# Depthwise convolutions, key norm and decay series: operands taken from and kept in PSUM

## The chip, the cores and the metric

One core of a Trainium2 chip runs the whole program in one launch. The metric is the device time of one execution in microseconds. The engines are named as in the profile: PE (matmul; PEld its weight load), DVE (VectorE), ACT (ScalarE), POOL (GpSimd), SP (its DMA queue). SBUF is the on-chip memory that all engines use; PSUM is the small one that PE writes its products to, in 8 banks of 512 fp32 columns. POOL has no PSUM operand in this kernel; DVE and ACT have.

## What is computed

A two-layer encoder on 256 tokens of width 1024. Each layer has a mixer of three parallel branches (dense attention A, neighbourhood attention B, gated DeltaNet C) and a top-2 mixture of 32 experts. The change lies in branch C's convolution and decay, and in branch A's key norm:

```python
p = h @ w_in
(aq, ak, av, bq, bk, bv, cq, ck, cv, cz, cbf, cbb, caf, cab, gate) = _split_cols(p, IN_SPLITS)
...
k = _axial_rope(_rms(k, k_g), tables)
...
qkv = jax.nn.silu(_short_conv(jnp.concatenate([q, k, v], axis=-1), conv_w))
...
g = -jnp.exp(A_log[d].astype(F32)) * jax.nn.softplus(aa.astype(F32) + dt_bias[d].astype(F32))
```

`_short_conv` is a centred convolution of 5 taps along the tokens, channel by channel. `g` is the log decay of the chunked delta rule, of 16 values per token partition.

## The kernel before

A layer runs as a mixer stage and an expert stage. The mixer's input projection takes `w_in` in column blocks in the order of `ORDER` (L50): first a block of gates (`ga0`), then branch C's queries and keys (`cqk`), its gate and decay inputs (`cz`), its values (`cv`), branch A's keys and values (`akv`), its queries (`aq`), and so on. Each block comes in four units of 256 rows. A unit is loaded by SP, its rounded half `uh_...` is made by ACT and the remainder `ul_...` by DVE or POOL (`split`, L185; `POOL`, L42, lists the units whose remainder POOL makes), and PE takes three products of them (`mm3`, L188). Four buffers of each kind go round.

PE's order is pinned as the program is recorded: `projections` (L1040) yields after every few products, and `pump` (L328) lets side lines put their matmuls between them. `delta_line` (L607), `key_line` (L581) and `query_line` (L593) are such lines. The order on DVE, ACT and POOL is a scheduler's, and each of them works its own queue strictly in order.

The steps that the prediction follows:

- `conv` (L536): ACT copies a PSUM bank of products into SBUF (`ring0` or `ring1`, both in the place H), DVE applies 5 taps to each of two channel groups (`ts`, then four `stt`), ACT takes a tanh into the ring, DVE forms `cs`. It runs three times, for `cqk` twice and for `cv`.
- `norm_rope` (L554): ACT copies the products to a ring, squares them, DVE reduces, POOL raises to the power -1/2 (`rsqrt`, L228), DVE scales, POOL multiplies by the sines, DVE by the cosines and adds. For the keys (`which` = 1) it runs for two token tiles. The second tile uses `ring0` and `ring1`, as the third convolution uses `ring0`.
- The decay series (L630 to L646): some 25 DVE instructions of 16 columns in the tile `gap`, which end in `g`. POOL then multiplies `g` with triangles three times (L656), PE forms `eb` and `db` from them (L662, L685), and then transposes the keys (`kTA`, L590).
- The query's norm (L596) follows the last `aq` product; PE transposes its result as `qTA` (L602).

PSUM banks come from three pools (`BANKS`, L155): `acc` with 3, `one` with 1, `s` with 4.

Of the kernel before, what the change touches and what calls it, by code (L numbers as in the profile page):

```python
# [15 lines left out]
OP = mybir.AluOpType  # L16
# [5 lines left out]
S = 256  # L22
# [91 lines left out]
def kernel(ctx: ExitStack, tc: tile.TileContext, a: dict, out: bass.AP):  # L114
# [45 lines left out]
    def tt(eng, o, x, y, op):  # L160
        return eng.tensor_tensor(out=o, in0=x, in1=y, op=op).ins  # L161
# [145 lines left out]
    def mixer(l, fetch, norm):  # L307
# [74 lines left out]
        def of(n, *shape):  # L382

            names = "abcd"[:len(shape)]
            w = where[n][:, :int(np.prod(shape))]
            if len(shape) == 1:
                return w
            return w.rearrange(f"p ({' '.join(names)}) -> p {' '.join(names)}", **dict(zip(names, shape)))
# [146 lines left out]

        def conv(i, b):  # L536

            bv = of(f"ring{i % 2}", 2, S)
            with tc.high_priority(offset=PRI):
                A.copy(bv.rearrange("p m s -> p (m s)"), b)  # L540
            y = of(f"cy{i % 2}", 2, S)
            for m in range(2):
                ch = 2 * i + m
                ts(V, y[:, m], bv[:, m], cw[:, ch, 2:3], OP.mult)
                for j in (0, 1, 3, 4):
                    s = j - 2
                    t0, t1 = max(0, -s), S - max(0, s)
                    stt(y[:, m, t0:t1], bv[:, m, t0 + s:t1 + s], cw[:, ch, j:j + 1], y[:, m, t0:t1],
                        OP.mult, OP.add)
            A.activation(bv, y, AF.Tanh)  # L550
            stt(cs[i], bv, 1.0, y, OP.add, OP.mult)


        def norm_rope(b, t, n, which, dst, name):  # L554

            turn = 2 * (t + which) % 4
            x, y = of(f"ring{turn}", 512), of(f"ring{turn + 1}", 512)
            A.copy(x[:, :n * 64], b)
            xv = x8(x[:, :n * 64])
            sq = y  # L560
            A.activation(sq[:, :n * 64], x[:, :n * 64], AF.Square)
            rs = of(f"rs{t}", 8)
            V.tensor_reduce(out=rs[:, :n], in_=x8(sq[:, :n * 64]), axis=AX.X, op=OP.add)
            rsqrt(rs[:, :n], rs[:, :n], 1.0 / 64.0, 1e-6, n)
            tt(V, xv, xv, rs[:, :n, None].to_broadcast([128, n, 64]), OP.mult)
            yv = x8(y[:, :n * 64])
            s5 = gc_[:, which, 1, t].rearrange("p (a b e) -> p a b e", a=2, b=2)
            for b_ in range(2):
                o = y[:, :n * 64].rearrange("p (h a b e) -> p h a b e", a=2, b=2, e=16)[:, :, :, b_]
                i0 = x[:, :n * 64].rearrange("p (h a b e) -> p h a b e", a=2, b=2, e=16)[:, :, :, 1 - b_]  # L570
                i1 = s5[:, None, :, b_].to_broadcast([128, n, 2, 16])
                tt(G, o, i0, i1, OP.mult)
            tt(V, xv, xv, gc_[:, which, 0, t:t + 1].to_broadcast([128, n, 64]), OP.mult)
            tt(V, dst, xv, yv, OP.add)
# [32 lines left out]
        def delta_line(vbank, zb):  # L607
# [19 lines left out]

                return ap8.rearrange("p (d h) -> p d h", d=2)[:, :, None, :].to_broadcast([128, 2, 2, 4])

            xx, ax, ee, rr, ss, pp, acc, g = (sc[:, i] for i in range(8))  # L630
            tt(V, xx.rearrange("p (d t h) -> p d t h", d=2, t=2), ba[:, 1], dh(al[:, 1]), OP.add)
            stt(ax, xx, -1.0, xx, OP.mult, OP.max)
            A.activation(ee, ax, AF.Exp, scale=-1.0)
            ts(V, rr, ee, 2.0, OP.add)
            V.reciprocal(rr, rr)
            tt(V, ss, ee, rr, OP.mult)
            tt(V, pp, ss, ss, OP.mult)
            ts(V, acc, pp, 1.0 / 19.0, OP.mult)
            for k in range(17, 1, -2):
                stt(acc, acc, 1.0 / k, pp, OP.add, OP.mult)  # L640
# [399 lines left out]
        def projections():  # L1040
            for i, n in enumerate(ORDER):
                if n == XFREE:
                    free("X")
                if n == RSPAWN:
                    spawn("router", router_line(), RLAG)
                if n == "cqk":
                    bs = [bank("acc", f"cqk{l}{i}") for i in range(2)]
                    for u in range(4):
                        uh, ul = take()
                        for k in range(2):  # L1050
                            chan(bs, uh, ul, u, k, 0, 4)
                            yield
                    conv(0, bs[0])
                    conv(1, bs[1])
                elif n == "cz":
                    zb = [bank("acc", f"cz{l}{t}") for t in range(2)]
                    for u in range(4):
                        uh, ul = take()
                        for k in range(2):
                            for t in range(2):  # L1060
                                mm3(zb[t][:, :272], act(2 * u + k, t), (uh[:, k], ul[:, k]),
                                    u == 0 and k == 0, u == 3 and k == 1)
                            yield
                elif n == "cv":
                    vbank = bank("acc", f"cv{l}")
                    for u in range(4):
                        uh, ul = take()
                        for k in range(2):
                            chan([vbank], uh, ul, u, k, 0, 2)
                            yield  # L1070
                    spawn("delta", delta_line(vbank, zb))
                elif n == "akv":
                    spawn("key", key_line((yield from token_major(n, 256))))
                elif n == "aq":
                    spawn("query", query_line((yield from token_major(n, 512))))
                elif n == "bqk":
                    bs = [bank("acc", f"bqk{l}{i}") for i in range(2)]
                    for u in range(4):
                        uh, ul = take()
                        for k in range(2):  # L1080
                            chan(bs, uh, ul, u, k, 0, 4)
                            yield
                    for i in range(2):
                        A.copy(bqk[:, i].rearrange("p m s -> p (m s)"), bs[i])
                elif n == "bv":
                    bs = yield from token_major(n, 256)
                    for t in range(2):
                        A.copy(vB[:, t], bs[t])
                    done.add("b")
                else:  # L1090
                    bs = yield from (token_major(n, 512) if i else tile_by_tile(n))
                    if i == 0:
                        small_inputs()
                    key = n[1], int(n[2])
                    if key not in gth:
                        pair = gc if n[1] == "c" else st((128, 2, 2, 512), "gb", f"gb{l}")
                        gth[n[1], 0], gth[n[1], 1] = pair[:, 0], pair[:, 1]
                    for t in range(2):
                        A.activation(gth[key][:, t], bs[t], AF.Tanh, scale=0.5)
# [531 lines left out]
```

## Time and profile before

| what | value |
|---|---|
| median of 3 runs | 1470.63 us (1470.15 to 1471.12) |
| the profiled execution, its own time | 1470.02 us |
| its span, first to last instruction | 1468.4 us |
| PE busy | 1341.5 us, 91% of the span |
| DVE, ACT, POOL busy | 632.3, 403.8, 266.2 us |
| mean granted clock of PE | 0.972 |
| HBM read | 476.40 MB |

The 1.6 us between the time and the span lie before the first and behind the last instruction. Times in the views count from the start of the span. A timeline row gives start, duration, engine, line, operation, output, inputs and shape; in brackets stands how long the engine was idle before and what ended that. `placeA`, `placeB`, ... are 2048-column places in SBUF that hold several named tiles; which one is meant follows from the line. The first mixer fills about 0 to 283 us, the second about 740 to 1010 us.

### The profile page before, as it was taken

Reading aid. Unit: us, or ns where it says so; the run is one execution under the profiler, and the core shown is the slowest. Engines: PE = TensorE matmul, PEld = TensorE weight load, DVE = VectorE, ACT = ScalarE, POOL = GpSimd, SP = SyncE. Lnnn points to the kernel's source line nnn. Section 1 sums busy time; section 2 is a strip of 40 time slices with the busy share of each in tenths; the row PEclk is TensorE's granted clock in tenths of the full one; section 3 lists DMA queues with packets and bytes.
Section 4 is the critical chain, followed back from the end, with each engine's and each line's share of the span. In section 5 each row is a group of like instructions: output and inputs, shape, how many; then the busy total and the mean of one; then the engine's idle time right before and its main releaser. Section 6 shows DMA issues by size and latency. Waiting matters only on the chain. (4 is left out here: it accounts for less than half of the span.)

```text
span 1468.4 us, 23692 instructions
## 1 busy us (share of the span) xinstructions
PE 1341.5 (91%) x9708; PEld 893.4 (61%) x9708; DVE 632.3 (43%) x1214; ACT 403.8 (28%) x769; POOL 266.2 (18%) x327
## 2 busy tenths in 40 slices
PE   6889999799998999999678799997999899999986
PEld 5768777555554555555367677774555556555542
DVE  6887667622221222222169875775222212222213
ACT  3445543211111111211134455332211111111111
POOL 4485304300000000000036743033000000000000
PEclk9999999899999999999979899999999999999999
DMA  7535779699999999999655457796999999999995
GB/s 232 168 123 148 226 244 344 233 405 419 419 419 417 419 419 419 419 419 420 266 163 156 138 141 255 242 355 239 407 418 419 418 418 419 420 419 419 419 419 212
DMA packets 114533, 479.89 MB, mean 327 GB/s; under 512 B 25168, under 2 KB 38000, under 8 KB 65520
## 3 DMA queue, kind: packets, MB, share of 16 engines
q1 hardware_dynamic: 112464, 471.85, 82.7%
q0 software_dynamic: 1376, 5.24, 1.0%
q8 instruction: 81, 1.33, 0.4%
q10 hardware_dynamic: 576, 1.18, 0.2%
q14 instruction: 36, 0.29, 0.1%
HBM read 476.40 MB, written 1.84 MB: 326 GB/s over the span
## 5 line engine op out<-in xcount | busy, mean ns | idle before, releaser
L176 PE MATMUL h<-w,h 128*64 128x256 f32 x2016 | 232.7, 387 | 21.7 <-PEq L1382 9.5
L176 PEld LDWEIGHTS h<-w,h 128*64 128x64 f32 x2016 | 144.0, 139 | 100.3 <-issue 16.6
L170 DVE SCALAR_TENSOR_TENSOR hid<-hid,h 128x256 f32<-128x256 f32 x64 | 27.0, 421 | 401.3 <-ACT hid L1473 401.3
L170 DVE SCALAR_TENSOR_TENSOR op<-mo,rt,op 64x512 fp32r<-64x512 f32 x128 | 95.9, 749 | 223.0 <-ACT op L1500 222.0
L1500 ACT ACTIVATE op<-mo,rt 64x512 fp32r<-64x512 f32 x128 | 87.4, 683 | 314.5 <-PE mo L176 275.1
L176 PE MATMUL mo<-w,hidT 128*64 128x512 f32 x720 | 164.3, 595 | 3.5 <-DMA w<-in_w_dram 2.2
L161 POOL TENSOR_TENSOR W<-P,rt 128x128 f32<-128x128 f32 x64 | 24.2, 399 | 785.2 <-PE PT L182 710.3
L1473 ACT ACTIVATE hid<-h 128x256 f32<-128x256 f32 x64 | 24.6, 385 | 402.3 <-PE h L176 402.3
L176 PEld LDWEIGHTS mo<-w,hidT 128*64 128x64 f32 x720 | 50.7, 137 | 89.1 <-issue 77.3
L176 PE MATMUL h<-w,xg 128*64 128x256 f32 x864 | 96.9, 380 | 2.3 <-ACT h L1448 2.3
L176 PE MATMUL h<-wl,h 128*64 128x256 f32 x768 | 86.3, 381 | 2.1 <-ACT h L1448 1.4
L176 PEld LDWEIGHTS h<-w,xg 128*64 128x64 f32 x864 | 61.0, 137 | 33.6 <-ACT h L1448 3.4
L176 PE MATMUL mo<-wl,hidT 128*64 128x512 f32 x304 | 69.8, 597 | 2.5 <-DMA wl<-in_w_dram 2.5
L176 PEld LDWEIGHTS h<-wl,h 128*64 128x64 f32 x768 | 53.9, 137 | 29.9 <-ACT h L1448 2.1
L176 PE MATMUL my<-op,PT 128*128 128x512 f32 x256 | 69.7, 412 | 2.1 <-ACT op L1500 1.4
L176 PE MATMUL xg<-P,hh 128*128 128x256 f32 x256 | 56.4, 303 | 5.8 <-DVE P L161 5.8
L176 PEld LDWEIGHTS my<-op,PT 128*128 128x128 f32 x256 | 45.5, 188 | 25.4 <-issue 11.5
L176 PEld LDWEIGHTS xg<-P,hh 128*128 128x128 f32 x256 | 40.8, 196 | 29.6 <-issue 29.5
L176 PE MATMUL xg<-P,hl 128*128 128x256 f32 x256 | 52.7, 288 | 0.0
L176 PE MATMUL h<-wl,xg 128*64 128x256 f32 x416 | 47.7, 382 | 3.2 <-DMA wl<-in_w_dram 1.6
L176 PEld LDWEIGHTS mo<-wl,hidT 128*64 128x64 f32 x304 | 20.6, 137 | 37.3 <-issue 29.8
L176 PE MATMUL wo<-uh_wo,ym 128*128 128x512 f32 x128 | 41.4, 395 | 0.0
(436 smaller groups left out, 2463.9 us busy)
## 6 DMA issues: line engine op xcount, KB each, us to landing
w<-in_w_dram SPq DMA_DIRECT2D x268, 1024.0 KB, 19.9
wl<-in_w_dram SPq DMA_DIRECT2D x112, 1024.0 KB, 19.9
w_gb<-in_w_in_dram SPq DMA_DIRECT2D x16, 512.0 KB, 3.7
w_gc<-in_w_in_dram SPq DMA_DIRECT2D x16, 512.0 KB, 4.5
w_wo<-in_w_out_dram SPq DMA_DIRECT2D x16, 512.0 KB, 4.8
w_ga<-in_w_in_dram SPq DMA_DIRECT2D x14, 512.0 KB, 4.7
w_cqk<-in_w_in_dram SPq DMA_DIRECT2D x8, 512.0 KB, 3.7
w_aq<-in_w_in_dram SPq DMA_DIRECT2D x8, 512.0 KB, 4.5
```

Source lines behind the costliest of these rows:

```text
L161: return eng.tensor_tensor(out=o, in0=x, in1=y, op=op).ins
L170: return V.scalar_tensor_tensor(out=o, in0=x, scalar=s, in1=y, op0=op0, op1=op1)
L176: ins = T.matmul(o, l, r, start=start, stop=stop, skip_group_check=True).ins
L1473: A.activation(u, b[:, :256], AF.Tanh, scale=0.5)
L1500: A.activation(hi, src, AF.Copy, scale=w)
```

## The change

The three convolutions read their products where PE left them and write their tanh back there; the copy into the ring is gone. The key norm squares and scales straight from PSUM and writes the scaled key to the ring; the query norm stays as it was. The decay series keeps its reciprocal, one of two copies of its quotient and its running sum in a PSUM bank `sb`, and forms the square from one factor in PSUM and one in SBUF, which is one instruction more. The banks of `cqk` and `cv` come from the pool `s` in place of `acc`.

```diff
         def conv(i, b):
 
-            bv = of(f"ring{i % 2}", 2, S)
-            with tc.high_priority(offset=PRI):
-                A.copy(bv.rearrange("p m s -> p (m s)"), b)
+            bv = b.rearrange("p (m s) -> p m s", m=2)
             y = of(f"cy{i % 2}", 2, S)
...
             turn = 2 * (t + which) % 4
             x, y = of(f"ring{turn}", 512), of(f"ring{turn + 1}", 512)
-            A.copy(x[:, :n * 64], b)
             xv = x8(x[:, :n * 64])
+            raw = x8(b) if which else xv
+            if not which:
+                A.copy(x[:, :n * 64], b)
             sq = y
-            A.activation(sq[:, :n * 64], x[:, :n * 64], AF.Square)
+            A.activation(sq[:, :n * 64], b if which else x[:, :n * 64], AF.Square)
             rs = of(f"rs{t}", 8)
             V.tensor_reduce(out=rs[:, :n], in_=x8(sq[:, :n * 64]), axis=AX.X, op=OP.add)
             rsqrt(rs[:, :n], rs[:, :n], 1.0 / 64.0, 1e-6, n)
-            tt(V, xv, xv, rs[:, :n, None].to_broadcast([128, n, 64]), OP.mult)
+            tt(V, xv, raw, rs[:, :n, None].to_broadcast([128, n, 64]), OP.mult)
...
-            xx, ax, ee, rr, ss, pp, acc, g = (sc[:, i] for i in range(8))
+            xx, ax, ee, ss, pp, g = (sc[:, i] for i in range(6))
+
+            sb = bank("s", f"sb{l}")
+            rr, sq_, acc = (sb[:, 16 * i:16 * i + 16] for i in range(3))
             tt(V, xx.rearrange("p (d t h) -> p d t h", d=2, t=2), ba[:, 1], dh(al[:, 1]), OP.add)
             stt(ax, xx, -1.0, xx, OP.mult, OP.max)
             A.activation(ee, ax, AF.Exp, scale=-1.0)
             ts(V, rr, ee, 2.0, OP.add)
             V.reciprocal(rr, rr)
+            tt(V, sq_, ee, rr, OP.mult)
             tt(V, ss, ee, rr, OP.mult)
-            tt(V, pp, ss, ss, OP.mult)
+            tt(V, pp, sq_, ss, OP.mult)
             ts(V, acc, pp, 1.0 / 19.0, OP.mult)
...
-                    bs = [bank("acc", f"cqk{l}{i}") for i in range(2)]
+                    bs = [bank("s", f"cqk{l}{i}") for i in range(2)]
...
-                    vbank = bank("acc", f"cv{l}")
+                    vbank = bank("s", f"cv{l}")
```

PE's order is the same before and after. On the other three the scheduler places things anew. First DVE, in the middle of the series, in the kernel before (`gap` is the series, `placeA` the third convolution's sum, `placeH` the ring, `placeS` small tiles with the taps, `ul_aq` a remainder of a query unit):

```order
L161 TENSOR_TENSOR gap_83<-gap_83 128x16
L165 TENSOR_SCALAR placeA_99<-placeH_105,placeS_108 128x256
L161 TENSOR_TENSOR gap_83<-gap_83 128x16
L165 TENSOR_SCALAR placeA_99<-placeH_105,placeS_108 128x256
L165 TENSOR_SCALAR gap_83<-gap_83 128x16
L170 SCALAR_TENSOR_TENSOR placeA_99<-placeH_105,placeS_108,placeA_99 128x254
L170 SCALAR_TENSOR_TENSOR gap_83<-gap_83 128x16
L170 SCALAR_TENSOR_TENSOR placeA_99<-placeH_105,placeS_108,placeA_99 128x254
L186 TENSOR_TENSOR ul_aq_657<-w_aq_571,uh_aq_656 128x1024
```

The first query remainder stands behind the quotient, the square and one step of the series, and each instruction around it has both tensors in SBUF. The same stretch with the change:

```order
L165 TENSOR_SCALAR placeA_99<-cv_495,placeS_108 128x256
L170 SCALAR_TENSOR_TENSOR placeC_100<-cqk_276,placeB_98 128x512
L186 TENSOR_TENSOR ul_akv_638<-w_akv_550,uh_akv_637 128x512
L170 SCALAR_TENSOR_TENSOR placeG_106<-placeG_106,cz_421 128x256
L170 SCALAR_TENSOR_TENSOR placeG_106<-placeG_106,cz_422 128x256
L186 TENSOR_TENSOR ul_aq_656<-w_aq_569,uh_aq_655 128x1024
L167 TENSOR_SCALAR placeS_108<-placeS_108 128x16
L165 TENSOR_SCALAR sb_588<-gap_83 128x16
L170 SCALAR_TENSOR_TENSOR placeA_99<-cv_495,placeS_108,placeA_99 128x254
L638 RECIPROCAL sb_588<-sb_588 128x16
```

The remainder now stands ahead of the whole series, and the third convolution's first tap ahead of it, on the bank `cv` that PE must have finished. Second POOL, from the last query remainder to the end of the keys, in the kernel before (L232 is the power, `placeH` the ring, `placeG` and `placeC` the triangles):

```order
L186 TENSOR_TENSOR ul_aq_737<-w_aq_672,uh_aq_736 128x1024
L232 TENSOR_TENSOR placeS_108<-placeS_108,mhalf 128x2
L161 TENSOR_TENSOR placeH_105<-placeH_105,placeA_99 128x4x16 x2
L161 TENSOR_TENSOR placeG_106<-gap_83,placeK_109 128x512 x2
L161 TENSOR_TENSOR placeC_100<-gap_83,placeK_109 128x512
L232 TENSOR_TENSOR placeS_108<-placeS_108,mhalf 128x2
```

and with the change:

```order
L186 TENSOR_TENSOR ul_aq_734<-w_aq_671,uh_aq_733 128x1024
L232 TENSOR_TENSOR placeS_108<-placeS_108,mhalf 128x2
L161 TENSOR_TENSOR placeH_105<-placeH_105,placeA_99 128x4x16 x2
L161 TENSOR_TENSOR placeG_106<-gap_83,placeK_109 128x512
L232 TENSOR_TENSOR placeS_108<-placeS_108,mhalf 128x2
L161 TENSOR_TENSOR placeG_106<-gap_83,placeK_109 128x512
L161 TENSOR_TENSOR placeC_100<-gap_83,placeK_109 128x512
L161 TENSOR_TENSOR placeH_105<-placeH_105,placeA_99 128x4x16 x2
```

The second key tile's power has moved ahead of the second and third triangle. Its sine products stay behind all three.

## Rows read from the trace of the kernel before

**Rows 1.** Windows: stretch, length, PE, PEld, DVE, ACT, POOL busy, clock, DMA share, GB/s
```profile
40.00:80.00 40.00, 35.16 (x215) 30.08 (x213) 36.95 (x76) 18.16 (x33) 23.61 (x16) 0.96 0.53 158
80.00:120.00 40.00, 32.87 (x214) 29.10 (x214) 33.35 (x69) 17.72 (x29) 27.66 (x21) 0.87 0.43 129
120.00:160.00 40.00, 39.23 (x228) 30.55 (x226) 28.15 (x49) 24.43 (x52) 24.06 (x48) 1.00 0.64 180
...
280.00:300.00 20.00, 18.51 (x143) 13.04 (x143) 3.96 (x10) 2.25 (x6) 1.10 (x3) 0.88 0.53 184
...
500.00:600.00 100.00, 98.52 (x722) 58.00 (x720) 24.89 (x48) 18.57 (x39) 2.27 (x6) 1.00 1.01 419
```

**Rows 2.** Waits of PE, 0 to 270 us: in total, times, longest
```profile
PE qTA L182 <- DVE placeE L161: 4.9, 2, 3.5
PE aq L176 <- DVE ul_aq L186: 3.2, 1, 3.2
PE kTA L182 <- ACT gap L668: 2.3, 1, 2.3
```

**Rows 3.** Timeline of PE, three places in layer 1, then two in layer 2
```profile
53.45 0.28 PE L176 MATMUL akv<-uh_akv,placeT 128*128 128x256 f32 x1
...
82.19 0.66 PE L182 MATMUL kTA<-cst,placeG 128*128 128x128 f32 x4 [2.34 <-ACT gap L668]
...
109.01 0.90 PE L182 MATMUL qTA<-cst,placeE 128*128 128x128 f32 x3 [3.53 <-DVE placeE L161]
...
811.93 0.66 PE L182 MATMUL kTA<-cst,placeG 128*128 128x128 f32 x4 [1.73 <-ACT gap L668]
...
838.69 0.90 PE L182 MATMUL qTA<-cst,placeE 128*128 128x128 f32 x3 [3.38 <-DVE placeE L161]
```

**Rows 4.** Timeline of DVE, 60 to 86 us
```profile
60.74 2.35 DVE L170 SCALAR_TENSOR_TENSOR gap<-gap 128x16 f32<-128x16 f32 x1
...
63.41 1.21 DVE L186 TENSOR_TENSOR ul_aq<-w_aq,uh_aq 128x1024 fp32r<-128x1024 f32 x1
...
72.32 0.17 DVE L165 TENSOR_SCALAR gap<-gap 128x16 f32<-128x16 f32 x1
...
74.75 1.01 DVE L165 TENSOR_SCALAR gap<-gap,placeK 128x16 f32<-128x16 f32 x1
...
85.08 0.68 DVE L161 TENSOR_TENSOR placeB<-placeB,placeK 128x512 f32<-128x512 f32 x1
```

**Rows 5.** Timeline of POOL, 60 to 76 us
```profile
60.38 2.69 POOL L186 TENSOR_TENSOR ul_aq<-w_aq,uh_aq 128x1024 fp32r<-128x1024 f32 x1 [1.28 <-ACT uh_aq L186]
...
71.34 0.73 POOL L232 TENSOR_TENSOR placeS<-placeS,mhalf 128x2 f32<-128x2 f32 x1 [3.52 <-DVE gap L170]
72.55 1.13 POOL L161 TENSOR_TENSOR placeH<-placeH,placeA 128x64 f32<-128x64 f32 x2 [0.47 <-DVE gap L165]
73.64 2.09 POOL L161 TENSOR_TENSOR placeG<-gap,placeK 128x512 f32<-128x512 f32 x2
```

**Rows 6.** Timeline of ACT: the second key tile's copy in and copy out
```profile
73.53 0.27 ACT L558 COPY placeH<-akv 128x128 f32<-128x128 f32 x1 [0.74 <-DVE placeC L170]
...
81.72 0.30 ACT L585 COPY placeG<-placeG 128x128 f32<-128x128 f32 x1 [2.50 <-DVE placeG L161]
```

**Rows 7.** Timelines of DVE and POOL at 116.7 us: one operand in PSUM beside POOL
```profile
116.68 0.28 DVE L161 TENSOR_TENSOR placeC<-placeF,gr 128x128 f32<-128x128 f32 x1
...
116.71 1.29 POOL L161 TENSOR_TENSOR placeA<-placeC,placeK 128x512 f32<-128x512 f32 x1 [5.38 <-DVE placeC L161]
```

**Rows 8.** Groups of DVE by form, whole span: count, busy us, mean ns, idle before
```profile
L170 DVE SCALAR_TENSOR_TENSOR gap<-gap 128x16 f32<-128x16 f32 x22 | 12.4, 565 | 0.1
...
L170 DVE SCALAR_TENSOR_TENSOR placeA<-placeH,placeS,placeA 128x254 f32<-128x254 f32 x16 | 7.6, 476 | 0.0
...
L170 DVE SCALAR_TENSOR_TENSOR placeH<-s_b,placeE 128x256 f32<-128x256 f32 x16 | 6.0, 415 | 0.1
...
L170 DVE SCALAR_TENSOR_TENSOR lg<-lg,stats,bwr 128x32 f32<-128x32 f32 x4 | 1.0, 254 | 0.0
```

## The prediction, made blind

> **What bounds the kernel now.** I read the windows first. In the expert stage the DMA share is 1.01 at 419 GB/s, so that stage is bound by loading its weights. In the mixer the share is about half, and PE works 39 of 40 us from 120 us on, but only 35 and 33 of 40 between 40 and 120 us, with DVE busy for 37 and 33 [rows 1]. So the mixer has slack on PE in one stretch, and DVE is full there. Between the stages, at 280 to 300 us, the DMA share is 0.53: the prefetched experts are waiting and nothing is queued for memory. Whatever the mixer saves therefore starts the expert stream earlier, and its fixed length ends earlier by as much.
>
> The waits say what PE stands for in that stretch: the query transpose 4.9 us, the first query product 3.2, the key transpose 2.3, nearly all of it on DVE [rows 2]. The PE timeline then shows which of them count. From the key transpose of layer 1 to that of layer 2 it is 729.74 us, and from query transpose to query transpose 729.68, though the waits ahead of them differ [rows 3]. So the arrival of keys and queries sets the time, not the waits before: a wait at the first query product that goes away only moves PE sooner to the key transpose.
>
> Last, DVE and POOL side by side. A series step of 16 columns takes 2.35 us at 60.74, and POOL's remainder runs from 60.38 to 63.07: DVE ends as POOL does [rows 4, 5]. A step without such company takes 0.17 [rows 4], yet 22 steps average 0.565 [rows 8]. DVE instructions with two tensors in SBUF wait out POOL's. Those with one tensor in PSUM do not: at 116.68 one takes 0.28 while a POOL product starts at 116.71 and lasts 1.29 [rows 7].
>
> **The change, part by part.** *Removed:* five ACT copies per layer (three convolution banks, two key tiles). ACT is busy 18 of 40 us [rows 1]; by itself that is worth nothing, since ACT's casts there wait for PE, DVE or a transfer. What counts is that the second key tile no longer needs the ring: its copy at 73.53 waited for the third convolution's last DVE instruction [rows 6]. *Banks:* `eb` and the three `db` now take over the four banks of `cqk`, `cv` and `sb`. They need `g`, which DVE makes after the last read of each of these banks, so no wait is added: nothing. *The extra product* of the series: 0.17 us on DVE, counted below.
>
> *Step one, the time of `g`.* The first tap of the third convolution waits for PE to end `cv`, now 53.45, where the first key product starts [rows 3]; with POOL unhindered a little earlier, so I take 53.0. Behind it stand a 512-column step (0.68), two gate steps and the tap (0.42 each, the 256-column PSUM row), half a remainder (0.6) and the first query remainder (1.21): 3.8, so 56.8 [rows 4, 8]. From there to `g` the new DVE order has 19 instructions of 16 columns or fewer at 0.17 = 3.2, nine convolution steps at 0.42 = 3.8, one of 512 columns 0.68, four key steps of 128 columns at 0.42 or less = 1.7, and four remainders at 1.21 = 4.8. That is 14.2, and `g` is ready at 71.0, against 72.3 [rows 4]. The four remainders are the part that can still wait for POOL, and each needs PE to have freed its buffer. First gain: 1.3, if PE is not late for `eb`, and without its wait at the first query product it is not.
>
> *Step two, from `g` to the key transpose.* Now it is 9.9 us (72.3 to 82.19), because the second key tile starts at 73.53 and one half of the decay is held up for 1.01 [rows 3, 4, 6]. With the change the chain is POOL's: three triangles at 1.05 = 3.1, the power 0.73 between them, two sine products 1.13 [rows 5], then two DVE steps (0.6), the copy out (0.30) and six hand-overs at 0.2, about the 0.17 between that copy's end and the transpose [rows 3, 6]: 7.1. The key transpose comes at 78.1 instead of 82.19. Gain so far: 4.1.
>
> *Step three, from there to the query transpose.* Before, DVE starts the masks of branch C 2.9 us behind the key transpose (85.08), as the decay factors and one remainder stand ahead [rows 3, 4]. With the change these are placed before the last key step, and the masks can start when ACT has the exponentials, about 0.6 behind the transpose (an exponential of 512 columns, put at DVE's 0.68 for that width, starts with the hand-over to PE): 2.3 sooner. I take 2.2, since the query's squares on ACT may then come last. All that follows to the query transpose (109.01) is the same DVE and POOL queue, moved as a whole. PE, only 4.1 earlier, still waits there, for 4.9 − 2.2 = 2.7. Gain per layer: 6.3.
>
> The rest of the mixer is PE work that follows the query transpose at the same distance, and the solve on POOL that starts from it moves along. The clock is 0.96 and 0.87 in the two windows [rows 1], low after the idle stretches; one shorter stretch may give back a microsecond, one longer (PE waiting for `g`) take it: nothing. The second layer repeats the first [rows 3]. Two layers: 12.6, and 1470.02 − 12.6 = 1457.4 for the profiled execution. The median of the runs is 0.6 above that execution, so I forecast 1458.
>
> [...] The nearest PSUM row, 256 columns, takes 415 ns, and the SBUF row of 254 columns 476 [rows 8]: PSUM is no dearer there. [...]
>
> **The rivals.**
> *Small PSUM steps are dear.* No row shows a 16-column step in PSUM. The nearest, 32 columns read and written in PSUM, takes 0.254 [rows 8] against 0.17. If all 30 PSUM instructions between 53 us and `g` cost 0.08 more, `g` is 2.4 later: gain 3.9 per layer, 1462. For it: the row is the only one of that size. Against: the larger ones are not dearer.
> *Slower.* If a dependent step through PSUM costs about as much as a row of 512 columns, 0.68 [rows 4], the 17 chained steps of the series are 0.5 dearer each, 8.7 in all. The key transpose is then 4.6 later than now, step three gives 2.2 back, and two layers lose 5: 1475. It decides from 0.37 more per step on (6.3 / 17). Nothing in the trace is that dear, and the steps alternate with convolution steps that hide part of it.
> *PSUM operands take turns with POOL all the same.* Then `g` stays at 72.3 and only the ring's release counts: 2.8 + 2.2 per layer, 1460. Rows 7 speak against it.
> *Nothing arrives.* If the expert stream were waiting for memory already in the mixer, or a later wait took the gain back, it is 1470. Against: the DMA share of 0.53 before the stream, and a PE that is full from 120 us on [rows 1].
> *More.* If DVE's backlog goes altogether, all three waits vanish, 10.4 per layer [rows 2]: 1449.
>
> **How the numbers follow.** Forecast with the rival at 1460, 1453 to 1461: 0.58. Small steps dear, 1461 to 1466: 0.18. More, 1444 to 1452: 0.11. Nothing: 0.07. Slower: 0.06. Runs of this kernel differ by 0.07%, and a measurement can tell about 0.2%, 2.9 us, from no change. Faster: 0.58 + 0.18 + 0.11 = 0.87; same 0.07; slower 0.06. The range 1449 to 1465 leaves out no change, slower, and the outer ends of the two neighbours of the forecast.
>
> **What would show it.** Right: series steps and convolution steps at 0.2 and 0.45 with no 2 us outliers; no wait at the first query product; the key transpose near 78 and the query transpose near 102.7, still waiting; the same distances in layer 2. Step one is wrong if `g` is not near 71, two if it takes other than 7 us to the key transpose, three if DVE's masks do not follow within 1 us. The whole is wrong if the series' PSUM steps exceed 0.5, or if the expert stage grows by what the mixer loses.

## The result and the profile after

The changed kernel takes 1455.13 us (median of 4 runs, 1453.57 to 1456.89) against 1470.63: a ratio of 0.9892, 95% interval 0.9878 to 0.9905, so 15.5 us less. The profiled execution took 1453.57 us with a span of 1451.9. The forecast was 1458 and its range held the time.

The windows of [rows 1], in the kernel after:

```profile
40.00:80.00 40.00, 37.02 (x227) 32.28 (x226) 36.25 (x94) 20.04 (x37) 22.44 (x20) 0.91 0.63 194
80.00:120.00 40.00, 36.28 (x257) 32.73 (x256) 32.60 (x62) 18.41 (x34) 24.33 (x17) 0.91 0.39 117
...
280.00:300.00 20.00, 18.52 (x150) 11.01 (x151) 4.69 (x10) 3.50 (x8) 0.00 (x0) 1.00 0.93 335
```

PE works 37.0 and 36.3 of 40 us, where it worked 35.2 and 32.9. DVE is hardly less busy: it does more in the same time. From 280 us on the expert stream already runs (DMA share 0.93, before 0.53).

PE's timeline, places that answer to [rows 3], then the first of its waits up to 270 us behind the loads at the program's start, to be read with [rows 2]:

```profile
52.26 0.28 PE L176 MATMUL akv<-uh_akv,placeT 128*128 128x256 f32 x1
...
70.71 2.74 PE L176 MATMUL eb<-gap,placeK 128*128 128x8 f32 x12 [2.98 <-DVE gap L165]
73.29 3.63 PE L176 MATMUL db<-placeG,placeK 128*128 128x512 f32 x4
...
77.61 0.60 PE L182 MATMUL kTA<-cst,placeG 128*128 128x128 f32 x4
...
101.52 0.90 PE L182 MATMUL qTA<-cst,placeE 128*128 128x128 f32 x3 [3.53 <-DVE placeE L161]
...
822.46 0.55 PE L182 MATMUL qTA<-cst,placeE 128*128 128x128 f32 x3 [2.54 <-DVE placeE L161]
```

```profile
PE qTA L182 <- DVE placeE L161: 3.5, 1, 3.5
...
PE eb L176 <- DVE gap L165: 3.0, 1, 3.0
```

The query transpose comes 7.49 us sooner in layer 1 (109.01 to 101.52), and 16.23 in layer 2 (838.69 to 822.46). That is nearly the whole gain: the span is 16.5 shorter. Some 0.5 us of it is an earlier start of this execution (PE's first products begin at 10.02 instead of 10.56) and not the change. The waits at the first query product and at the key transpose are gone; one at `eb` is new.

DVE's timeline after, for [rows 4]:

```profile
51.79 1.17 DVE L165 TENSOR_SCALAR gap<-gap 128x16 f32<-128x16 f32 x1
...
62.10 0.17 DVE L170 SCALAR_TENSOR_TENSOR sb<-sb,gap 128x16 f32<-128x16 f32 x1
62.22 1.05 DVE L167 TENSOR_SCALAR placeS<-placeS 128x2 f32<-128x2 f32 x1
...
69.08 1.22 DVE L186 TENSOR_TENSOR ul_ga<-w_ga,uh_ga 128x1024 fp32r<-128x1024 f32 x1
...
70.49 0.16 DVE L165 TENSOR_SCALAR gap<-gap 128x16 f32<-128x16 f32 x1
...
77.58 0.69 DVE L161 TENSOR_TENSOR placeB<-placeB,placeK 128x512 f32<-128x512 f32 x1 [1.45 <-ACT placeB L690]
```

`g` is at 70.49 (72.32 before), the first mask (a triangle multiplied into branch C's decay factors) at 77.58 (85.08). From `g` to the mask it is 7.09 us instead of 12.76. Three remainders of the gate units, the last of them the row at 69.08, now stand ahead of `g`; before, all three stood between `g` and the masks (75.68, 79.36 and 81.60, 1.2 us each). ACT shows the other half. First two rows of the kernel before, then four of after:

```profile
77.97 0.30 ACT L585 COPY placeG<-placeG 128x128 f32<-128x128 f32 x1 [2.89 <-DVE placeG L161]
...
81.92 0.22 ACT L668 ACTIVATE gap<-eb 128x64 f32<-128x64 f32 x1
```

```profile
69.11 0.30 ACT L585 COPY placeG<-placeG 128x128 f32<-128x128 f32 x1 [0.88 <-DVE placeG L161]
73.48 0.22 ACT L672 ACTIVATE gap<-eb 128x64 f32<-128x64 f32 x1 [4.08 <-PE eb L176]
...
76.17 0.30 ACT L585 COPY placeG<-placeG 128x128 f32<-128x128 f32 x1 [0.19 <-DVE placeG L161]
76.95 0.60 ACT L690 ACTIVATE placeB<-db 128x512 f32<-128x512 f32 x1 [0.49 <-PE db L176]
```

Before, ACT copied both key tiles out (77.97, and 81.72 of [rows 6]) ahead of the exponential of `eb`, which PE had ready at 77.2 and which ran at 81.92; ahead of each of these copies ACT stood for DVE (2.89 and 2.50 us). After, the first key tile is done ahead of `g`, the exponential follows `eb` at once, and the second tile comes behind it.

Where DVE found the room stands in its groups by form, 36 to 83 us, of before and then of after:

```profile
L170 DVE SCALAR_TENSOR_TENSOR gap<-gap 128x16 f32<-128x16 f32 x11 | 6.2, 561 | 0.0
L170 DVE SCALAR_TENSOR_TENSOR placeB<-placeH,placeS,placeB 128x255 f32<-128x255 f32 x4 | 4.0, 991 | 0.0
L170 DVE SCALAR_TENSOR_TENSOR placeB<-placeH,placeS,placeB 128x254 f32<-128x254 f32 x4 | 3.9, 995 | 0.0
```

```profile
L170 DVE SCALAR_TENSOR_TENSOR placeB<-cqk,placeS,placeB 128x254 f32<-128x254 f32 x4 | 1.9, 474 | 0.0
L170 DVE SCALAR_TENSOR_TENSOR placeB<-cqk,placeS,placeB 128x255 f32<-128x255 f32 x4 | 1.9, 473 | 0.0
...
L170 DVE SCALAR_TENSOR_TENSOR sb<-sb,gap 128x16 f32<-128x16 f32 x10 | 1.7, 171 | 0.0
```

The second convolution loses 4.1 us (7.9 to 3.8), the series 4.5. Both were waits for POOL (experiments 1, 2 and 8), and POOL waited as well. Its remainders of the `cv` units in the kernel before, and the first of the same three after:

```profile
44.95 7.13 POOL L186 TENSOR_TENSOR ul_cv<-w_cv,uh_cv 128x512 fp32r<-128x512 f32 x3 [9.64 <-ACT uh_cv L186]
```

```profile
44.41 1.29 POOL L186 TENSOR_TENSOR ul_cv<-w_cv,uh_cv 128x512 fp32r<-128x512 f32 x1 [9.45 <-ACT uh_cv L186]
```

### The profile page after: what moved, and what is told of

Its sections match the earlier page's. It is cut to its first block, busy times and chain, and to the rows that moved or that the text cites. A ratio compares the mean times of both kernels' runs of the same rounds, so it can differ in the third digit from the quotient of the medians.

```text
span 1451.9 us, 23681 instructions
## 1 busy us (share of the span) xinstructions
PE 1337.3 (92%) x9708; PEld 893.7 (62%) x9708; DVE 618.6 (43%) x1216; ACT 400.5 (28%) x759; POOL 254.7 (18%) x327
```

## The experiments

**Theory:** the operands in PSUM free DVE of POOL; with that room, work that stood behind `g` moves ahead of it. **Rivals:** the ring's release of the second key tile alone; the order on ACT; a wait that only moves to the next instruction. PE's first products begin at 10.0 to 11.2 us in these profiles, so a few tenths between two of them are the start. From the masks to the query transpose of layer 1 it was 23.8 to 24.0 us in the runs of experiments 1 to 10, but for 23.1 in the first and 23.4 in the fifth; so the masks tell when the queries come.

**1. The convolutions alone** (`conv_only`): the kernel before, with the convolutions' part of the diff.

```diff
-            bv = of(f"ring{i % 2}", 2, S)
-            with tc.high_priority(offset=PRI):
-                A.copy(bv.rearrange("p m s -> p (m s)"), b)
+            bv = b.rearrange("p (m s) -> p m s", m=2)
...
-                    bs = [bank("acc", f"cqk{l}{i}") for i in range(2)]
+                    bs = [bank("s", f"cqk{l}{i}") for i in range(2)]
```

> Only the three convolutions read PSUM; series and key norm as before. Theory (port): DVE steps with two operands in SBUF wait out POOL's, one operand in PSUM avoids it. Then the convolution steps all take 0.47 us, the ring is free early, but the series keeps one or two steps of some 2 us beside POOL's query remainders; g comes 2 us later than with the whole change and the key and query transposes too: 1459 us. Rival (only the ring's release counts, the places of operands do not): 1455, as the whole change. Rival (the series carries the gain): 1468.

Measured 1456.67 us, 0.9904 [0.9888, 0.9919]. DVE's timeline:

```profile
58.79 1.48 DVE L161 TENSOR_TENSOR gap<-gap 128x16 f32<-128x16 f32 x1
...
61.72 2.37 DVE L161 TENSOR_TENSOR gap<-gap 128x16 f32<-128x16 f32 x1
...
72.09 0.16 DVE L165 TENSOR_SCALAR gap<-gap 128x16 f32<-128x16 f32 x1
...
73.97 2.06 DVE L186 TENSOR_TENSOR ul_ga<-w_ga,uh_ga 128x1024 fp32r<-128x1024 f32 x1
...
79.31 0.69 DVE L161 TENSOR_TENSOR placeB<-placeB,placeK 128x512 f32<-128x512 f32 x1
```

The convolutions bring 14 of the 15.5 us, although the series still waits (1.48, 2.37) and `g` is only 0.2 sooner than before, which is the start (10.36 against 10.56). One gate remainder is left behind `g` instead of three, and the mask comes 7.2 us behind it. The time lies between the theory's 1459 and the 1455 of the first rival and does not choose between them; experiments 5 and 6 do. The edit also takes the copies away: DVE's idle time ahead of the first tap falls from 1.5 us (behind ACT's copy) to 0.9 (behind PE), so that the first copy is worth some 0.6 us and not the 4.1 above.

**2. The series alone** (`series_only`): the kernel before with the bank `sb` and the steps in it.

```diff
-            xx, ax, ee, rr, ss, pp, acc, g = (sc[:, i] for i in range(8))
+            xx, ax, ee, ss, pp, g = (sc[:, i] for i in range(6))
+
+            sb = bank("s", f"sb{l}")
+            rr, sq_, acc = (sb[:, 16 * i:16 * i + 16] for i in range(3))
...
+            tt(V, sq_, ee, rr, OP.mult)
             tt(V, ss, ee, rr, OP.mult)
-            tt(V, pp, ss, ss, OP.mult)
+            tt(V, pp, sq_, ss, OP.mult)
```

> Only the decay series keeps operands in PSUM; convolutions and key norm go through the ring as before. Theory (port): the series' steps take 0.17 us, but the convolution steps that stand between them meet POOL's remainders instead and take 2 us; the ring is not released; 1468 us, g within 1 us of its time before. Rival (the series' stalls are the cause): g 4 us earlier, 1462.

Measured 1469.48, 0.9995 [0.9986, 1.0003]: nothing. Every step in the bank takes 0.17 (the reciprocal 0.27), but `g` is at 73.99, 1.7 later than before and not within 1 as expected. The waits went to the taps beside it (at 60.26 one of 2.57 us with two tensors in SBUF, at 64.95 one of 2.38 with a single one), and one remainder and the third convolution's last step moved ahead of `g`.

**3. All but the series** (`no_series`): the changed kernel with that part undone.

```diff
...
-            rr, sq_, acc = (sb[:, 16 * i:16 * i + 16] for i in range(3))
+            xx, ax, ee, rr, ss, pp, acc, g = (sc[:, i] for i in range(8))
...
-            tt(V, pp, sq_, ss, OP.mult)
+            tt(V, pp, ss, ss, OP.mult)
```

> The changed kernel with the series back in SBUF; convolutions and key norm stay on PSUM. DVE's order stays nearly the same. Theory: two series steps of 1.5 and 2.4 us come back beside POOL's query remainders, g is some 1.7 us later than with the whole change, the query transpose 1 us, and the time is that of the run with the convolutions alone: 1457 us. If the key norm alone is worth something, it lies below 1456.7; rival (the series' place is worth nothing): 1455.

Measured 1456.91, 0.9907 [0.9892, 0.9922], no different from the convolutions alone: the key norm's part can't be measured. `g` is at 72.26, 1.8 later than with the change, and the query transpose 2.05 later; without the later start (10.40) that is 1.4 and 1.7, which is what the series brings in layer 1 once the convolutions are in PSUM. In the time it shows as 1.8 us, and the two intervals overlap.

**4. One operand in PSUM is enough** (`one_operand`): the changed kernel with the sum back in SBUF and the square in PSUM in its place.

```diff
-            xx, ax, ee, ss, pp, g = (sc[:, i] for i in range(6))
+            xx, ax, ee, ss, acc, g = (sc[:, i] for i in range(6))
...
-            rr, sq_, acc = (sb[:, 16 * i:16 * i + 16] for i in range(3))
+            rr, sq_, pp = (sb[:, 16 * i:16 * i + 16] for i in range(3))
```

> The changed kernel with the places of two of the series' tiles exchanged: the square (pp) in PSUM, the running sum in SBUF, so that every step reads one tensor from SBUF and one from PSUM and writes to SBUF. Theory (one input in PSUM is enough): all steps 0.17 us beside POOL, 1455 us as the changed kernel. Rival (the sum's write or read in SBUF takes turns with POOL too): steps of 2 us beside POOL's remainders, 1457 or more.

Measured 1456.07, 0.9909 [0.9895, 0.9923], as the change. A step beside POOL's remainder, which runs from 60.69 to 63.57:

```profile
62.69 0.16 DVE L170 SCALAR_TENSOR_TENSOR gap<-gap,sb 128x16 f32<-128x16 f32 x1
```

Its output lies in SBUF; the step with its output in the bank took 0.17 beside POOL (62.10 of after), and steps with both inputs in SBUF took 1.48 and 2.37 (experiment 1). So here the one input in PSUM took the wait away, and the place of the output made no difference.

**5. The ring alone** (`ring_only`): the kernel before, the second key tile in two places of its own.

```diff
-            x, y = of(f"ring{turn}", 512), of(f"ring{turn + 1}", 512)
+            x, y = (of("Zc", 256), of("Zd", 256)) if which and t else (of(f"ring{turn}", 512), of(f"ring{turn + 1}", 512))
```

> The kernel before, with the second key tile in two other tiles that are free then (Zc, Zd) in place of the ring; nothing in PSUM is read that was not. Forecast's split: g stays near 72.3 (the series' 2 us steps remain), the key transpose comes 2.8 us after it sooner and the masks 2.2 sooner than that: 1460 us. Rival (the late key tile is only a symptom of DVE's backlog): 1468 to 1470.

Measured 1467.55, 0.9986 [0.9976, 0.9996]. But the scheduler put the halves of `g` at 79.03, behind the second tile, so that the keys' and masks' times here are not the ring's alone; a second kernel held the halves at their place.

**6. The ring, with the halves kept ahead** (`ring_first`): the edit of experiment 5, and

```diff
-                ts(V, sc[:, c2], g, C("half")[:, c2:c2 + 1], OP.mult)
+                with tc.high_priority(offset=PRI):
+                    ts(V, sc[:, c2], g, C("half")[:, c2:c2 + 1], OP.mult)
```

> The kernel before with the second key tile outside the ring, as in ring_only, and the two halves of the decay placed on DVE right behind g, as the changed kernel has them. If the ring's release is what brings keys and queries sooner (the forecast's steps two and three): key transpose 7.1 us after g, masks with it, 1459 us. Rival (DVE's backlog: the stalls of the convolutions push three gate remainders behind g, and those stand ahead of the masks): the key transpose comes sooner, the masks start 10 to 12 us after g as now, 1465 us.

Measured 1468.46, 0.9984 [0.9975, 0.9993]. DVE's timeline, then ACT's:

```profile
80.56 1.23 DVE L186 TENSOR_TENSOR ul_ga<-w_ga,uh_ga 128x1024 fp32r<-128x1024 f32 x1 [0.18 <-ACT uh_ga L186]
...
84.02 0.69 DVE L161 TENSOR_TENSOR placeB<-placeB,placeK 128x512 f32<-128x512 f32 x1
```

```profile
79.28 0.30 ACT L585 COPY placeG<-placeG 128x128 f32<-128x128 f32 x1 [2.86 <-DVE placeG L161]
...
80.43 0.22 ACT L669 ACTIVATE gap<-eb 128x64 f32<-128x64 f32 x1
```

The key transpose is 1.5 us sooner (80.70), the masks 1.1, as the gate remainders still stand ahead of them: 11.7 behind `g`, as the rival had it. The release by itself is worth some 2 us of the program by the medians (this profile's own execution was the longest of the 11, 1471.48). What the release is worth once DVE is free, no run shows: the edit of experiment 1 frees the ring too.

**7. No second key tile** (`no_key2`): the kernel before, the second key tile copied and not normed.

```diff
...
+                if t == 0:
+                    norm_rope(bs[t][:, :128], t, 2, 1, kA[:, t, :, 0], f"k{l}{t}")
...
+                else:
+                    for e in range(2):
+                        A.copy(kA[:, t, :, e], x8(bs[t][:, :128]))
```

> The kernel before, without the norm and rope of the second key tile (that part of the computation is left out: ACT copies its products as they are). New theory (the second key tile stands at the head of ACT's and DVE's queues: the decay's exponentials are queued behind its copy out on ACT, the masks behind them): the exponential of eb starts within 1 us of eb's end instead of 4.7 us behind it, the masks come 4 to 5 us sooner (near 80.5), the query transpose too, 23.9 after the masks; 1460 us. Rival (the three gate remainders behind g hold the masks): masks near 83, 1466. Second rival (work on POOL, not the queue: 2.1 us less in each layer): 1466 with the masks where they are.

Measured 1465.07, 0.9969 [0.9957, 0.9981]. ACT's timeline:

```profile
78.60 0.30 ACT L586 COPY placeG<-placeG 128x128 f32<-128x128 f32 x1 [3.77 <-DVE placeG L161]
...
79.75 0.22 ACT L672 ACTIVATE gap<-eb 128x64 f32<-128x64 f32 x1
```

With the second tile's work gone altogether, the first one takes its place at the head of ACT's queue, and the three gate remainders are still behind `g` (76.30, 78.49, 79.87). The exponential follows `eb`, which ends at 79.03, within 1 us, as the theory wanted, but the mask comes at 83.34 and not near 80.5: that is the first rival (83, 1466). Leaving out work that the change keeps brings a third of what the change brings, so the second tile as such was not the obstacle.

**8. Two query remainders off POOL** (`pool_off`): the kernel before, DVE makes them.

```diff
-POOL = (1, 2, 5, 13, 14, 15, 17, 18, 21, 23, 50, 62)
+POOL = (1, 2, 5, 13, 14, 15, 17, 18, 50, 62)
```

> The kernel before, with the two query remainders of POOL (units 21 and 23) made on DVE. Theory (port): no series step beside them takes more than 0.3 us; DVE saves two waits of 2.2 us and pays two remainders of 1.21, so g comes some 2 us sooner in each layer, the ring stays as it was: 1466 us (1463 to 1470). Rival (the 2 us steps come from something else than POOL, such as the chain of dependent small steps): they stay, DVE has 2.4 us more, 1475.

Measured 1464.35, 0.996 [0.9945, 0.9975]. The step that took 2.35 us [rows 4] stands on DVE's timeline as

```profile
60.46 0.16 DVE L170 SCALAR_TENSOR_TENSOR gap<-gap 128x16 f32<-128x16 f32 x1
```

with POOL idle (from 58.81 to 69.33) and both tensors in SBUF. POOL's company was the cost: even 2.4 us more work per layer on DVE (two remainders of 1.21) is cheaper.

**9. The same edit on the changed kernel** (`after_pool_off`).

> The changed kernel with POOL's two query remainders (units 21 and 23) made on DVE, as pool_off did to the kernel before. Theory (both take away the same waits of DVE for POOL): what pool_off won there (5.8 us) is not won again; the waits left beside those remainders are 0.8, 1.1 and 0.9 us in a layer against 2.4 us more work: 1455 us (1453 to 1457). Rival (the two add up): 1449.

Measured 1460.31, 0.9934 [0.9919, 0.9949], 5.2 us slower than the change, where the theory had 1455 and its rival 1449. `g` is 2.6 later, the masks 3.4. The sign is turned: here, with operands in PSUM, POOL's remainders cost DVE less than they relieve it of. Waits that the expectation counted as removed stayed. DVE, then POOL:

```profile
57.04 1.26 DVE L167 TENSOR_SCALAR placeS<-placeS 128x16 f32<-128x16 f32 x1
```

```profile
56.06 2.21 POOL L161 TENSOR_TENSOR placeG<-placeG,placeK 128x512 f32<-128x512 f32 x1 [2.35 <-DVE placeG L170]
```

They belong to a product that POOL keeps; both end at 58.3.

**10. The last waits moved to PSUM too** (`scalar_psum`): the changed kernel, with the single-tensor steps and the halves reading the bank.

```diff
-            ts(V, beta, beta, 0.5, OP.mult, 0.5, OP.add)
+            ts(V, beta, bt, 0.5, OP.mult, 0.5, OP.add)
...
+            ts(V, xx, xp, 0.0, OP.max)
+            stt(ax, xx, 2.0, xp, OP.mult, OP.subtract)
...
-                ts(V, sc[:, c2], g, C("half")[:, c2:c2 + 1], OP.mult)
+                with tc.high_priority(offset=PRI):
+                    ts(V, sc[:, c2], g2, C("half")[:, c2:c2 + 1], OP.mult, -1.0, OP.mult)
```

> The changed kernel, where the single-tensor steps on the decay's path (the maximum with 0, the half tanh of beta, the two halves of g) read PSUM instead of SBUF, and the halves stand right behind g. Theory (DVE's steps with one tensor, SBUF to SBUF, wait for POOL as well: 1.17, 1.27 and 1.26 us in the changed kernel): they take 0.2 to 0.4, g comes 2 us sooner, the masks 1.5 us sooner in each layer, 1452 us. Rival (such a step has its wait from something else): their durations stay, 1455. Rival (the wait moves to the next remainder, which has both tensors in SBUF): durations fall and g does not move, 1455.

Measured 1463.18, 0.9952 [0.9935, 0.9968], 8 us slower than the change. The edited steps do fall to 0.16 and 0.17. DVE's timeline shows where the wait went:

```profile
58.02 1.92 DVE L161 TENSOR_TENSOR sb<-gap,placeS 128x16 f32<-128x16 f32 x1
...
60.76 3.27 DVE L186 TENSOR_TENSOR ul_aq<-w_aq,uh_aq 128x1024 fp32r<-128x1024 f32 x1
```

Each is the next instruction with two inputs in SBUF, and the series behind them starts later: `g` at 75.16, 4.7 behind the change.

**11 and 12. Filling PE's remaining waits.** `retimed` is the changed kernel with later due times for the side lines; `filled` keeps its first two, and moves the query line forward, with its products copied out at once, so that the ring and ACT's order change with it.

```diff
-    "delta": [15.03, 1.23, 3.7, 10.0, 0, 0.76, 53.51, 0, 0, 0.8, 0.24, 0.0, 0.52, 1.67, 1.37, 0, 2.87, 2.23, 0, 2.03, 1.99, 0, 2.87, 1.99, 0, 2.87, 6.3],
-    "key": [10.0],
-    "query": [16.22, 1.92, 1.92],
+    "delta": [17.0, 1.23, 3.7, 10.0, 0, 0.76, 53.51, 0, 0, 0.8, 0.24, 0.0, 0.52, 1.67, 1.37, 0, 2.87, 2.23, 0, 2.03, 1.99, 0, 2.87, 1.99, 0, 2.87, 6.3],
+    "key": [11.6],
+    "query": [22.5, 1.92, 1.92],
```

> The changed kernel with three numbers of the PE order raised (delta 15.03 to 17.0, key 10.0 to 11.6, query 16.22 to 22.5): the last two groups of query products and one of gate products stand ahead of the decay's small product, and 24 convolution-free projection products ahead of the query transposes. If PE's remaining waits (3.0 at the decay, 3.5 and 2.5 at the query transposes) are real losses, 5 to 6 us per layer go: 1444 us. Rival (the chain through POOL's solve then ends last, and PE waits at the solve's products instead): 1450. Rival (the queries' chain on POOL delays the solve): no gain, 1455.

```diff
-    "query": [16.22, 1.92, 1.92],
+    "query": [6.0, 18.0, 1.92, 1.92],
...
+            for t in range(2):
+                A.copy(qA[:, t].rearrange("p x d -> p (x d)"), bs[t])
+            yield
```

> The changed kernel with PE's waits filled: the last query products and three gate products ahead of the decay's small product, the query's products copied out at once (to their final place instead of the ring) and its norm recorded behind the branch C transposes, so that it does not go ahead of them as in the run with three numbers raised; the query transposes behind the grams. If PE's idle time before the decay only cost clock (its products run at half clock after 3 us of idling), the masks come 1 to 2 us sooner, gram and solve as well, and PE's 3.5 us wait is filled: 1449 us. Rival (the chain through POOL and the solve is all that counts and does not move): 1455. Rival (another order on DVE and POOL delays the branch C chain): 1460 or more.

Measured 1474.16, 1.0023 [1.0013, 1.0033], for the one and 1475.46, 1.0037 [1.0023, 1.0051], for the other: 19 and 20 us slower than the change. In `retimed` branch C's keys come behind the queries on DVE, and PE waits 3.1 for them. In `filled` all went as meant at first: branch C's Gram products (`gr`) start at 103.93 (104.9 with the change), those of its solve (`T`) at 154.7 (155.5). Its waits behind 200 us:

```profile
PE y0c L176 <- DVE ym L186: 2.4, 1, 2.4
...
PE y0c L176 <- ACT ym L186: 1.2, 1, 1.2
```

The mixer ends at 276.7 (`rk`), against 268.1. Both waits at `y0c` are absent from the change, and from 120 to 280 us PE is idle for 18.7 us against 10.8. I read this as the cover moved away: the products that filled the early gaps had stood beside the end of branch C's scan. That is not shown by itself, but in neither run was filling the wait at the query transpose a gain.

## Why the prediction was right, and where not

*The bound.* Right. From `rk`, the products of the router's ranking at the mixer's end (275.52 before, 268.12 after), to layer 2's first gate product (744.37, 736.88) it is 468.85 and 468.76 us: the expert stage kept its length, and what the mixer saved came out at the end. From layer 2's `rk` to the end it is 463.04 and 464.39, but the runs of all kernels here spread from 462.9 to 464.5, with no sign of the change. The arrival of the queries set the time, in layer 1 almost to the hundredth (masks to transpose 23.93 and 23.94). The equal distances of 729.7 us that the prediction took for this show only that layer 2 repeats layer 1; the constant way from the masks bears it out.

*Step one, `g` at 71.0.* It came at 70.49. Some 0.5 of the 1.8 us are the earlier start of the whole program, so the gain of 1.3 is met; PE was done with `cv` at 52.26, sooner than the 53.0 taken. The sum of 14.2 behind the first query remainder came out (56.27 to 70.49) by errors that cancel: three rows waited for POOL, some 2.8 us that the sum does not have (two steps with a single tensor at 56.27 and 62.22, and the remainder of 2.01 at 58.96), and the convolution steps took 0.47 and not 0.42; against this most rows start before the one ahead of them ends, 3.0 us in all, which the sum does not have either. And the step's place was mistaken: its four remainders were counted as a burden on `g`, but that they no longer stand behind `g` is where the gain lies. The room in DVE's queue went not into `g` but into work moved ahead of it, and experiment 1 gains 14 us with `g` where it was.

*Step two, 7.1 us to the key transpose.* Measured 7.12 (70.49 to 77.61), by another chain than the one summed. POOL's chain ran in the order that I summed, but was done sooner (the two sine products took 0.61 instead of 1.13, and the hand-overs little): the copy out ended at 76.47. What came last was PE, at a granted clock of 0.50 (70 to 76 us): `eb` and the first four `db` took 2.74 and 3.63 us where before they took 1.40 and 1.96. The prediction allowed that PE waiting for `g` could cost clock, but did not expect that wait; it is 2.98 at `eb`. So the term for the clock, "nothing", was wrong at this place, and the sum of 7.1 was met by luck. The windows of 66 to 74 us, first before, then after, show where each ran slow (the granted clock is the third number from the end):

```profile
66.00:70.00 4.00, 4.00 (x12) 3.13 (x11) 4.00 (x8) 0.00 (x0) 1.82 (x1) 0.57 0.73 251
70.00:74.00 4.00, 4.00 (x19) 3.25 (x19) 3.17 (x14) 2.01 (x4) 2.18 (x4) 1.00 0.78 259
```

```profile
66.00:70.00 4.00, 1.72 (x8) 1.11 (x6) 4.00 (x13) 2.20 (x5) 1.53 (x2) 0.98 0.77 232
70.00:74.00 4.00, 3.29 (x13) 3.06 (x14) 2.50 (x9) 0.22 (x1) 3.27 (x4) 0.50 0.61 205
```

Before, PE waited at the first query product (3.17 us), the low clock (0.50 from 67 to 69 us) fell on query products, and `eb` ran at 1.00 (70 to 80 us). After, the wait is at `eb` (2.98), and the low clock of 0.50 falls on the chain to the masks, 3.0 us dearer there. In both the low clock follows the wait; that the wait brings it is my reading, and no run isolates it. Over both windows of 40 us the mean is the same (0.96 and 0.87 before, 0.91 and 0.91 after): the clock was moved, not lost. The reason that I gave for step two, the release of the ring, does not carry it by itself (experiments 5 to 7).

*Step three, masks 0.6 behind the key transpose.* They start with it (77.58, 77.61), because ACT's first exponentials (75.38 and 76.95) do not wait for the transpose. That is 0.7 more than the 2.2 taken. Together with `g` 0.5 sooner this makes the query transpose 101.52 and not 102.7, and PE still waits there, 3.5 instead of 2.7. The 4.9 that the prediction reduced are two waits [rows 2], 1.42 at 105.19 and 3.53 at 109.01; the first is gone but for 0.2, the second as long as it was.

*Two layers alike.* This is the term that was mis-sized: 7.5 (7.0 without the start) and 8.7 instead of 6.3 each. In layer 2 `g` is 10.0 us sooner (802.08, 792.08), 2.5 beyond the shift from layer 1; the way to the masks is 5.4 shorter and that to the transpose 0.8.

*A term put at nothing.* The convolutions' copies were not worth nothing by themselves: without the first of them DVE idles 0.6 us less ahead of the first tap (experiment 1). How much of this reaches the masks is not shown.

*The rivals.* Small PSUM steps are not dear (0.17); that nothing arrives, or that it is slower, did not happen. That operands in PSUM take turns with POOL all the same is excluded by experiments 2 and 4 (0.17 and 0.16 beside POOL's remainders); [rows 7] could not do it, as DVE's step there starts 0.03 us ahead of POOL's. That the whole backlog goes (1449) is half true: two of three waits are gone, and one new one stands at `eb`.

*What is shown, and what stays open.* Shown: the series' steps with two inputs in SBUF waited for POOL (1.48 to 2.37 us beside its query remainders), and with one input in PSUM they do not (0.16 and 0.17; 1, 2, 4, 8), but why they wait for it (the "port" of the expectations) no run shows; freeing the convolutions is nearly all of the gain (1 to 3); the ring's release alone is not it (5 and 6), nor is the second key tile (7). That the gain passes through the three gate remainders and the first key tile, which now go ahead of `g`, is read from the order in every run: three remainders left between `g` and the masks gave 1465 to 1471 us, two 1464 to 1469, one 1457 twice, none 1455 and 1456, but also 1460 and 1463 where DVE had other work or waits ahead of `g` (experiments 11 and 12, with one, have another order on PE). It is not shown by itself: each edit made the scheduler order three queues anew, and no run holds that order fixed and changes the operands alone.

## What to carry to other kernels

Look for short VectorE instructions that end as a GpSimd instruction does: here an input left in PSUM took them out of its way (2.35 us to 0.17), and took the copy out as well. Judge the gain by what the freed queue then puts ahead of the critical step, not by the sum of the stalls: the series' 4.5 us per layer were worth nothing alone, as the waits moved to their neighbours, and the edit that took the convolutions' 4.1 away brought seven. And before filling a wait on TensorE, ask which later gap its filler was covering.

## What was not expected of the hardware

- Some instructions with a single tensor in SBUF wait for POOL too. The two `TENSOR_SCALAR` at 51.79 and 62.22 (16 and 2 columns) took 1.17 and 1.05 us and ended at 52.96 and 63.27; POOL's instructions beside them ended at 52.93 and 63.25. The `SCALAR_TENSOR_TENSOR` at 62.10 with an input in PSUM took 0.17 in between. POOL's row, and a DVE row beside it that reads a single tensor in SBUF and did not wait:

```profile
60.70 2.55 POOL L186 TENSOR_TENSOR ul_aq<-w_aq,uh_aq 128x1024 fp32r<-128x1024 f32 x1 [0.81 <-ACT uh_aq L186]
61.91 0.27 DVE L563 TENSOR_REDUCE placeS<-placeH 128x2 f32<-128x128 f32 x1
```

So the two operations differ here: 1.17 and 1.05 us for the `TENSOR_SCALAR`, 0.27 for the `TENSOR_REDUCE`. What tells them apart, no run shows. The prediction had only pairs of tensors wait.
- A tap with one tensor took longer from PSUM (471 ns against 346), one with two did not (470 against 476). Groups by form over the whole span, two of after, then the second's counterpart of before:

```profile
L170 DVE SCALAR_TENSOR_TENSOR placeA<-cv,placeS,placeA 128x254 f32<-128x254 f32 x8 | 3.8, 470 | 0.0
...
L165 DVE TENSOR_SCALAR placeA<-cv,placeS 128x256 f32<-128x256 f32 x4 | 1.9, 471 | 0.0
```

```profile
L165 DVE TENSOR_SCALAR placeA<-placeH,placeS 128x256 f32<-128x256 f32 x8 | 2.6, 346 | 3.0 <-ACT placeH L540 3.0
```

The first took 476 from SBUF [rows 8]. No run here shows the reason. The steps of the series with two tensors, of 16 columns, took 172 ns with an input in the bank, and 0.16 to 0.18 us from SBUF where POOL was idle.
- POOL pays as well: 7.13 us for three remainders beside the convolutions, 4.26 of them for one, before, and 1.29 to 1.30 each with the change.
